# A transformer block on one core: the softmax's sink term added a step later, a merge that begins with other products, and a new order of the last two pairs of products

## The chip, the core and the metric

The kernel runs on one core of a Trainium2 chip. Its engines are TensorE (PE; weight loads are listed apart as PEld), VectorE (DVE), ScalarE (ACT), GpSimd (POOL) and SyncE (SP, which here only issues DMAs). The metric is the time of one execution in microseconds (us) on the device. All times below are us from the start of the profiled span unless something else is said.

## What is computed

One layer over 1024 latent tokens and 256 context tokens of width 1024, everything in fp32: windowed attention with eight query heads on two key/value heads, beside a Fourier mixing; a gated merge of the two; then a gated feed-forward with a convolution of width 3. Cut to what the change touches:

```python
# attention: each block of 128 queries against up to 3 x 128 local keys and 256 context keys
p = softmax(concatenate([s_loc, s_ctx, sink_l], axis=-1), axis=-1)
o = einsum(p_loc, vw) + einsum(p_ctx, v_ctx)          # the sink takes weight and has no value
# merge
m = sigmoid(g_a) * (attn_o @ w_pa) + sigmoid(g_f) * (four_o @ w_pf)
x = x + gt1 * rmsnorm(m @ w_out, g_post1)
# feed-forward, last norm
u, gate = split(modulate(rmsnorm(x, g_pre2), sh2, sc2) @ w_up, 2)
x = x + gt2 * rmsnorm((silu(conv3(u)) * gate) @ w_down, g_post2)
```

## The kernel before, in words

**Products.** Every fp32 product is made of three PE passes: each operand is split into a high and a low half (`split`, L102: ACT copies the high half, `sub` on DVE or POOL forms the low one), and `mm3` (L106) issues high x high, high x low and low x high (L108 to L110). `tt` at L91 is the helper behind every add, subtraction and product of two tiles; nearly all of them run on DVE.

**Attention, about 330 to 517.** A `Unit` is one block of 128 queries of one key/value head (four heads); there are 16, and the digits of a name are block and head: unit 41 is block 4, head 1. `score` makes the scores of one head on PE, adds the mask and takes the row maximum on DVE (`p`, `mx`, L1199). `guard` (L1204) forms `nm`, minus the larger of maximum and sink, and `es` = sink + `nm`. `exp` (L1211) runs on ACT; its call for the first head first exponentiates `es`. `norm` (L1215) adds `es` to the sums, inverts, and scales the four `p` on POOL (L1219). `turn(j)` transposes one key tile of all heads on PE (`pp`, L1224) and splits it (`ph` on ACT, `pl` on DVE); `prod(j)` multiplies the halves with the values into `po` (L1235); `fold` copies half of `po` on ACT (`tp`) and adds it on DVE (`aT`). `step` (L1302) works on three units at once, in six rounds `g`: unit `c` is turned and multiplied, `b` gets its last three exponentials and its norm, `a` its scores, its guard and `exp(0)`. In round 3 the guard of `a` comes last; round 4 begins with `turn(4)` of `c`. The engines run in the order in which the code is written (`manual_schedule`). Each step also carries one product of the Fourier branch (`pf_tile`, result times `sgf`, stored to memory as `mf_d`), and every second step a weight split whose low half (`wlpf`) is made by POOL.

**Merge, from 517.** `PA` lists 16 output tiles `(j, h)`: 128 channels `j`, half `h` of the tokens. Each is a product of 12 matmuls (`pa_mm`), after which `pa_out` multiplies by the gate `sga` and adds `mf` on DVE, and splits the sum. Half `h` = 1 needs `ah`/`al` of the last query blocks. The first two entries are loaded ahead and run at the loop's end (`EARLY`); the loads of entries 2 to 4 are issued behind them, then `att_split(1, ...)` makes the last two `ah`/`al` pairs, and then the other entries follow. SP's queue carries loads and stores in the order in which they are written.

**Down, to the end.** The feed-forward runs in seven products per pair of tiles (P1 to P7, a scheme of Strassen's kind) of 9 or 12 matmuls; the last of them work in three PSUM banks X, Y, Z (`BANK`). X holds P1, P6, P7 and P4, of which ACT copies the first three out (`snP`, L392), each ahead of the next; Y holds P5 and P3. `wino_items` fixes the order: P1, P2, then P4 and P3 of the pair before, then P6, P5, P7; so the last pair's P4 and P3 end the program. Behind a pair's last sums, `finish` squares each half row with its sum (`d_square`, ACT), multiplies by the gate `G2` (`d_gate`, DVE), forms the inverse root in small steps (`rstd_steps`, L160), scales and adds the residual (`d_out`, L1778) and stores. `ssd` holds the sums of squares of the two halves. The last pair (rows i0 = 3 and i1 = 7) has its end written out by hand behind `run(14, M)`.

Of the kernel before, what the change touches and what calls it, by code (L numbers as in the profile page):

```python
# [63 lines left out]
def block_kernel(ctx: ExitStack, tc: tile.TileContext, t: dict, out: bass.AP, dbg: dict):  # L64
# [28 lines left out]
    def add(out, a, b, eng=None):  # L93
        return tt(out, a, b, ALU.add, eng)
# [44 lines left out]
    def tiny(name, n, bufs=4, dtype=F):  # L139
        return small.tile([P, n], dtype, tag=f"ty{n}", name=name, bufs=bufs)  # L140
# [95 lines left out]
    def wino(pairs, items, psf, hooks, slots=False, seng=None):  # L236

# [937 lines left out]
    class Unit:  # L1175
# [186 lines left out]
    with tc.manual_schedule():  # L1362
# [425 lines left out]
    def down_pair(c, m):  # L1788
        last = c == len(CH) - 1
        ld = {p: [d[m] for d in g_d[c, p]] + ([g_both[c, p][m]] if (c, p) in g_both else []) for p in STA}  # L1790

        half = set()

        def finish(i, n):

            first = i not in half
            half.add(i)
            if not first and m == NT // 2 - 1:
                return None

            def squares():
                d_square(i, n)
                d_gate(i, n)
                if first:
                    return None
                rs = rstd_steps(ssd[:, i, :], f"d{i}")
                return [(1, rs[0]), (2, rs[3]), (3, lambda: [rs[1](), d_out(i, 0, rs[2])] and None),
                        (4, lambda: d_out(i, 1, rs[2])), (6, lambda: [d_store(i, h) for h in range(2)] and None)]
            return [(1, squares)]

        def ev(q, pst, sn):
# [9 lines left out]
            y = yd[i, n]  # L1821
            if pst is None:
                add(y, y, sn)
                if last and q == 11:
                    x1_load(m)
                    x1_load(m + NT // 2)
                return None
            add(y, y, pst)
            return finish(i, n) if last else None
# [10 lines left out]
    items = wino_items(len(pairs), START)  # L1840
    pos = {it: k for k, it in enumerate(items)}
# [10 lines left out]
    def load_g2():  # L1852
        for h in range(2):
            G2.append(s(f"G2{h}"))
            load(out=G2[h], in_=gt_d[1, :, h * 512:(h + 1) * 512])

    at(32, lambda: seng.__setitem__(0, nc.gpsimd))
    at(pos[NF - 3, "P1"], lambda: seng.__setitem__(0, nc.vector))
    at(pos[NF - 1, "P3"] + 6, swap_misc)
    at(pos[NF + 12, "P1"], load_g2)  # L1860
    seng = [nc.vector]
    run, ahead, flush, due, pre, conv, sums, mm, evac, st = wino(pairs, items, ps, hooks, True, seng)
    with tc.manual_schedule():
# [200 lines left out]
        i0, i1 = NT // 2 - 1, NT - 1  # L2064
        evac_last = due[M].pop()
        due[M], rest = [], due[M]
        for fn in rest:
            fn()
        d_square(i1, 0)
        rs1 = rstd_steps(ssd[:, i1, :], f"d{i1}")  # L2070
        rs0 = rstd_steps(ssd[:, i0, :], f"d{i0}")
        rs1[0]()
        rs1[3]()
        d_gate(i1, 0)
        rs1[1]()
        assert not evac_last()
        d_square(i0, 1)
        d_out(i1, 1, rs1[2])
        d_store(i1, 1)
        rs0[0]()  # L2080
        rs0[3]()
        d_gate(i0, 1)
        for k in range(7):
            flush(M + k)
        assert not due, sorted(due)
        rs0[1]()
        for i, n, r in ((i0, 1, rs0), (i0, 0, rs0), (i1, 0, rs1)):
            d_out(i, n, r[2])
            d_store(i, n)
    miscD[0].release()  # L2090
# [76 lines left out]
```

## Time and profile before

| what | us |
|---|---|
| three runs, median (lowest to highest) | 1300.64 (1299.89 to 1301.2) |
| the profiled execution, its own time | 1300.34 |
| its span in the trace | 1298.6 |

The span is what the profile shows from the first to the last instruction; 1.74 us of the execution lie around it. The rows further down come from that one execution. PE takes a new matmul before the last has ended, so durations overlap: the distance of two starts is what a matmul costs a full row of them, and a longer distance is a stop. The granted clock of TensorE is 1.00 from 330 to 1265.

### The profile page before, as it was taken

To read this page: it belongs to the slowest core of one execution; us is meant where nothing else is said; L and a number is where in the kernel's file an instruction comes from. 1 tells how busy PE (TensorE), PEld (TensorE's weight loads), DVE (VectorE), ACT (ScalarE), POOL (GpSimd) and SP (SyncE) were. 2 spreads that over 40 slices of the span, in tenths; PEclk is the share of its full clock that TensorE was granted. 3 is DMA by queue.
4 is the path that set the end of the run, shared out by engine and by line. 5 is a ranking of instruction groups with operands and counts; after the bars stand their busy time and mean duration, and the time that the engine had idled before them with its cause. 6 is when DMAs were issued, how large, how long until landed. Compare 5 with 4: busy or idle time off the path is not lost.

```text
span 1298.6 us, 18497 instructions
## 1 busy us (share of the span) xinstructions
PE 1256.2 (97%) x5998; PEld 1022.1 (79%) x5998; DVE 1030.4 (79%) x1865; ACT 682.7 (53%) x1357; POOL 232.0 (18%) x191
## 2 busy tenths in 40 slices
PE   5999999999899999999999999999999999999996
PEld 3768777888878877788878888888888887888884
DVE  4867767875788996867889999999888877666767
ACT  7754337533667676344477555454444555544442
POOL 0001221100333333000000032544554200000000
PEclk9999999999999999999999999999999999999999
DMA  9997474604334343945213686687767778977983
GB/s 317 346 324 232 142 230 138 193 31 134 88 100 120 114 122 110 325 155 157 81 42 106 187 250 210 205 240 222 219 187 227 211 219 288 367 255 222 291 292 140
DMA packets 271573, 254.56 MB, mean 196 GB/s; under 512 B 16732, under 2 KB 206836, under 8 KB 271476
## 3 DMA queue, kind: packets, MB, share of 16 engines
q1 hardware_dynamic: 271476, 253.38, 62.5%
q8 instruction: 47, 0.77, 0.2%
q14 instruction: 50, 0.41, 0.1%
HBM read 179.65 MB, written 73.40 MB: 195 GB/s over the span
## 4 chain that ended last, share of the span: by engine, by line
PE 79%; DVE 13%; ACT 3%; issue 2%; DMA 1%; POOL 1%; SPq 0%; DVEq 0%; POOLq 0%; ACTq 0%
PE X_u L110 5%; PE X_u L109 5%; PE X_u L108 5%; PE X_d L110 3%; PE X_d L109 3%; PE X_d L108 3%; PE Y_u L110 3%; PE Y_u L108 3%; PE Y_u L109 3%; PE X_g L108 2%; PE X_g L109 2%; PE X_g L110 2%; DVE p L1199 2%; DVE pl L91 2%; PE y L110 2%
## 5 line engine op out<-in xcount | busy, mean ns | idle before, releaser
L91 DVE TENSOR_TENSOR lP_u<-A_u,hP_u 128x512 fp32r<-128x512 f32 x132 | 105.7, 805 | 22.6 <-ACT hP_u L330 20.8
L392 ACT COPY snP_u<-X_u 128x512 f32<-128x512 f32 x57 | 33.4, 585 | 128.5 <-PE X_u L110 128.5
L392 ACT COPY snP_d<-X_d 128x512 f32<-128x512 f32 x48 | 28.2, 587 | 97.8 <-PE X_d L110 93.7
L330 ACT CAST hP_u<-A_u 128x512 fp32r<-128x512 f32 x121 | 74.6, 619 | 1.9 <-PE Y_u L109 1.9
L1219 POOL TENSOR_SCALAR p<-p,sm 128x640 f32<-128x640 f32 (+1 forms) x64 | 48.3, 774 | 92.1 <-PE pp L1224 35.3
L103 ACT CAST ph<-pp 128x512 fp32r<-128x512 f32 x76 | 44.3, 584 | 22.3 <-PE pp L1224 21.0
L91 DVE TENSOR_TENSOR pl<-pp,ph 128x512 fp32r<-128x512 f32 x76 | 51.6, 681 | 2.5 <-ACT ph L103 2.0
L91 DVE TENSOR_TENSOR yd<-yd,snP_d 128x512 f32<-128x512 f32 x36 | 24.9, 691 | 34.1 <-ACT snP_d L392 33.9
L1213 ACT ACTIVATE p<-p,nm 128x640 f32<-128x640 f32 (+1 forms) x64 | 51.3, 802 | 0.7 <-DVE nm L1206 0.7
L91 POOL TENSOR_TENSOR A_u<-A_u,A_u 128x512 f32<-128x512 f32 x28 | 48.5, 1732 | 13.8 <-DVE lP_u L91 6.8
L1199 DVE CUSTOM_DVE_ANT_0 p<-ss,mask 128x640 f32<-128x640 f32 (+1 forms) x64 | 49.9, 781 | 0.0
L1224 PE MATMUL pp<-ident,p 128*128 128x128 f32 x304 | 46.6, 274 | 2.8 <-POOL p L1219 1.5
L1224 PEld LDWEIGHTS pp<-ident,p 128*128 128x128 f32 x304 | 37.2, 140 | 11.7 <-POOL p L1219 2.9
L1658 DVE SCALAR_TENSOR_TENSOR tb<-u,vec,tb 128x1024 f32<-128x1024 f32 x22 | 38.8, 1766 | 3.1 <-ACT tb L1655 3.1
L91 POOL TENSOR_TENSOR S_u<-A_u,A_u 128x512 f32<-128x512 f32 x14 | 24.1, 1722 | 89.3 <-DVE u L91 82.2
L1659 DVE SCALAR_TENSOR_TENSOR tb<-u,vec,tb 128x1024 f32<-128x1024 f32 x22 | 37.5, 1704 | 0.9
L1195 PE MATMUL ss<-kst,qs 128*128 128x384 f32 (+1 forms) x128 | 36.6, 367 | 1.3 <-DVE mx L1199 0.8
L91 DVE TENSOR_TENSOR lP_g<-A_g,hP_g 128x512 fp32r<-128x512 f32 x48 | 33.3, 701 | 5.2 <-ACT hP_g L103 4.3
L91 POOL TENSOR_TENSOR A_u<-S_u,A_u 128x512 f32<-128x512 f32 x14 | 18.7, 1333 | 102.6 <-DVE lP_u L91 89.2
L91 DVE TENSOR_TENSOR wB<-wB,wB 128x512 f32<-128x512 f32 x44 | 35.8, 814 | 0.0
L1235 PE MATMUL po<-pl,vst 128*128 128x512 f32 x76 | 31.3, 412 | 3.0 <-DVE pl L91 2.4
L320 ACT COPY snP_g<-X_g 128x512 f32<-128x512 f32 x24 | 14.1, 587 | 36.4 <-PE X_g L110 35.6
(888 smaller groups left out, 4359.5 us busy)
## 6 DMA issues: line engine op xcount, KB each, us to landing
A_u<-in_w_up SPq DMA_DIRECT2D x88, 256.0 KB, 4.4
wB<-in_w_down SPq DMA_DIRECT2D x44, 256.0 KB, 4.4
wa<-in_w_mod SPq DMA_DIRECT2D x36, 256.0 KB, 5.3
wt_dT<-wB SPq DMA_DIRECT2D x33, 256.0 KB, 2.2
wdB<-in_w_down SPq DMA_DIRECT2D x33, 256.0 KB, 4.6
wdT<-wt_dT SPq DMA_DIRECT2D x33, 256.0 KB, 3.1
A_g<-in_w_in SPq DMA_DIRECT2D x32, 256.0 KB, 5.1
ws<-in_w_mod SPq DMA_DIRECT2D x30, 256.0 KB, 6.0
```

Source lines behind the costliest of these rows:

```text
L91: return (eng or nc.vector).tensor_tensor(out=out, in0=a, in1=b, op=op)
L103: copy(hi, src)
L108: nc.tensor.matmul(ps, ah, bh, start=start, stop=False, skip_group_check=True)
L109: nc.tensor.matmul(ps, ah, bl, start=False, stop=False, skip_group_check=True)
L110: nc.tensor.matmul(ps, al, bh, start=False, stop=stop, skip_group_check=True)
L330: copy(st[j]["half", p][0], st[j][STA[p]])
L392: copy(d["s" + p], d["X"])
L1199: nc.vector.tensor_tensor_reduce(out=p_, in0=ssc[:, lo:768], in1=self.mk, op0=ALU.add, op1=ALU.max, scale=1.0, scalar=-3.0e38, accum_out=s ...
L1213: nc.scalar.activation(out=self.pt[g], in_=self.pt[g], func=AF.Exp, scale=SCALE, bias=self.m[:, g:g + 1], accum_out=self.sm[:, g:g + 1])
L1219: nc.gpsimd.tensor_scalar(out=self.pt[g], in0=self.pt[g], scalar1=self.sm[:, g:g + 1], scalar2=1.0, op0=ALU.mult, op1=ALU.mult)
L1224: nc.tensor.transpose(pp[:, g * P:(g + 1) * P], self.pt[g][:, j * P:(j + 1) * P], ident)
L1658: nc.vector.scalar_tensor_tensor(out=tb, in0=u[:, 0:1024], scalar=cw[0], in1=tb, op0=ALU.mult, op1=ALU.add)
```

## The change

There are four pieces. **(1)** The add that forms `es` and its exponential leave `guard` and `exp(0)` and go to a method of their own, `sink`, which `step` calls a step later, in round 1, when the unit has become `b`. **(2)** `PA` begins with the first three tiles of token half 0, then three of half 1. **(3)** `wino_items` runs the last two pairs each by itself, in the order P1, P2, P6, P5, P7, P3, P4; their sums are taken from PSUM one by one. **(4)** `rstd_steps` takes four small DVE operations behind the sums in place of six, one of them ahead of the second sum; `G2` is halved once, with changed sign, on ACT; the hand-written end follows the new order.

```diff
-    def rstd_steps(parts, name):
+    def rstd_steps(parts, name, other=0):
...
+        def early():
+            nc.vector.tensor_scalar(out=w, in0=parts[:, other:other + 1], scalar1=1.0 / D, scalar2=EPS, op0=ALU.mult, op1=ALU.add)
         def one():
-            add(v, parts[:, 0:1], parts[:, 1:2])
-            nc.vector.tensor_scalar(out=v, in0=v, scalar1=1.0 / D, scalar2=EPS, op0=ALU.mult, op1=ALU.add)
+            nc.vector.scalar_tensor_tensor(out=v, in0=parts[:, 1 - other:2 - other], scalar=1.0 / D, in1=w, op0=ALU.mult, op1=ALU.add)
...
-            nc.vector.tensor_scalar(out=n1, in0=n1, scalar1=-0.5, scalar2=1.5, op0=ALU.mult, op1=ALU.add)
-            mul(r2, r, n1)
+            nc.vector.scalar_tensor_tensor(out=r2, in0=n1, scalar=-3.0, in1=r, op0=ALU.add, op1=ALU.mult)
...
+            if i > n - own:
+                items.extend((j, p) for j, p in ([] if i > n - own + 1 else [(i - 1, "P1"), (i - 1, "P2"), (i - 2, "P4"), (i - 2, "P3")]))
+                items.extend((i - 1, p) for p in ("P1", "P2", "P6", "P5", "P7", "P3", "P4") if (i - 1, p) not in items)
+                continue
...
-            self.es, self.sm = tiny(f"es{self.nm}", 4, 16), tiny(f"sm{self.nm}", 4, 16)
-            add(self.es, snk[:, hs], self.m)
+            self.sm = tiny(f"sm{self.nm}", 4, 16)
+
+        def sink(self):
+            self.es = tiny(f"es{self.nm}", 4, 16)
+            add(self.es, snk[:, self.kv * GRP:self.kv * GRP + GRP], self.m)
+            nc.scalar.activation(out=self.es, in_=self.es, func=AF.Exp)
         def exp(self, g):
-            if g == 0:
-                nc.scalar.activation(out=self.es, in_=self.es, func=AF.Exp)
...
             if b and g < 3:
                 b.exp(g + 1)
+                if g == 1:
+                    b.sink()
...
-    PA = ((0, 0), (1, 0), (0, 1), (1, 1)) + tuple((j, h) for j in range(2, KT) for h in range(2))
+    PA = tuple((j, h) for h in range(2) for j in range(3)) + tuple((j, h) for j in range(3, KT) for h in range(2))
...
+    OWN = 2
+    items = wino_items(len(pairs), START, OWN)
...
+        for h in range(2):
+            nc.scalar.activation(out=G2[h], in_=G2[h], func=AF.Copy, scale=-0.5)
...
+        d_square(i1, 0)
+        two0()
+        d_out(i0, 1, r0)
+        d_store(i0, 1)
+        one1()
+        root1()
+        d_gate(i1, 0)
+        two1()
+        d_out(i1, 1, r1)
+        d_store(i1, 1)
+        d_out(i0, 0, r0)
+        d_store(i0, 0)
+        d_out(i1, 0, r1)
+        d_store(i1, 0)
```

How DVE's row of work changes in a step of the attention (unit 31 is `c`, 40 is `b`, 41 is `a`), before, from the guard of unit 41 on:

```order
L1206 SCALAR_TENSOR_TENSOR nm41_4615<-mx41_4539,nsnk_3209 128x4
L91 TENSOR_TENSOR es41_4617<-snk_3188,nm41_4615 128x4
L91 TENSOR_TENSOR pl314_4626<-pp314_4620,ph314_4625 128x512
L91 TENSOR_TENSOR sgf7_4397<-pf7_4564,sgf7_4397 128x512
L91 TENSOR_TENSOR aT10_3228<-po31_4588,tp31_4649 64x2x128 x2
L91 TENSOR_TENSOR pl400_4667<-pp400_4661,ph400_4666 128x512
L1199 ISA p500_4677,mx50_4671<-ss500_4672,mask_3186 128x640
L1199 ISA mx50_4671 128x1
L91 TENSOR_TENSOR pl401_4685<-pp401_4679,ph401_4684 128x512
```

and after, the same stretch and one row more:

```order
L1223 SCALAR_TENSOR_TENSOR nm41_4615<-mx41_4536,nsnk_3209 128x4
L91 TENSOR_TENSOR pl314_4624<-pp314_4618,ph314_4623 128x512
L91 TENSOR_TENSOR sgf7_4394<-pf7_4564,sgf7_4394 128x512
L91 TENSOR_TENSOR aT10_3228<-po31_4588,tp31_4646 64x2x128 x2
L91 TENSOR_TENSOR pl400_4664<-pp400_4658,ph400_4663 128x512
L1216 ISA p500_4674,mx50_4668<-ss500_4669,mask_3186 128x640
L1216 ISA mx50_4668 128x1
L91 TENSOR_TENSOR pl401_4682<-pp401_4676,ph401_4681 128x512
L91 TENSOR_TENSOR es41_4686<-snk_3188,nm41_4615 128x4
```

`es41` no longer stands between `nm41` and `pl314`; it follows `pl401` a step later. POOL's order is the same in both.

DVE's row at the start of the merge, before, from the last two low halves of the attention's output on:

```order
L91 TENSOR_TENSOR al21_5680<-aT11_3229,ah21_5679 128x512
L91 TENSOR_TENSOR al31_5684<-aT11_3229,ah31_5683 128x512
L91 TENSOR_TENSOR sga01_5667<-pa01_5762,sga01_5667 128x512
L91 TENSOR_TENSOR mf01_5668<-mf01_5668,sga01_5667 128x512
L91 TENSOR_TENSOR ml01_5797<-mf01_5668,mh01_5796 128x512
L91 TENSOR_TENSOR sga11_5671<-pa11_5777,sga11_5671 128x512
L91 TENSOR_TENSOR mf11_5672<-mf11_5672,sga11_5671 128x512
L91 TENSOR_TENSOR wlpa4_5814<-wpa4_5775,whpa4_5813 128x512
```

and after:

```order
L91 TENSOR_TENSOR al21_5680<-aT11_3229,ah21_5679 128x512
L91 TENSOR_TENSOR sga20_5667<-pa20_5762,sga20_5667 128x512
L91 TENSOR_TENSOR al31_5684<-aT11_3229,ah31_5683 128x512
L91 TENSOR_TENSOR mf20_5668<-mf20_5668,sga20_5667 128x512
L91 TENSOR_TENSOR ml20_5797<-mf20_5668,mh20_5796 128x512
L91 TENSOR_TENSOR sga01_5671<-pa01_5777,sga01_5671 128x512
L91 TENSOR_TENSOR mf01_5672<-mf01_5672,sga01_5671 128x512
L91 TENSOR_TENSOR wlpa4_5814<-wpa4_5775,whpa4_5813 128x512
```

The gate product of tile (2, 0), `sga20`, has come between `al21` and `al31`; before, both stood ahead of every gate product that was left. On PE tile (2, 0) runs first now, then (0, 1).

DVE's last rows, before, from the sum of P3 of the last pair for row 3 on (`yd31` and `yd71` take the bank Y, `yd70` the bank X):

```order
L91 TENSOR_TENSOR yd31_11557<-yd31_11557,Y_d33_13168 128x512
L1778 SCALAR_TENSOR_TENSOR yd71_11502<-yd71_11502,r2d7_13235,xf71_13090 128x512
L91 TENSOR_TENSOR vd3_13236<-ssd_5759 128x1
L166 TENSOR_SCALAR vd3_13236<-vd3_13236 128x1
L91 TENSOR_TENSOR yd31_11557<-yd31_11557,G21_12600 128x512
L172 RECIPROCAL rd3_13238<-sqd3_13237 128x1
L173 SCALAR_TENSOR_TENSOR n1d3_13239<-rd3_13238,vd3_13236 128x1
L174 TENSOR_SCALAR n1d3_13239<-n1d3_13239 128x1
L91 TENSOR_TENSOR r2d3_13240<-rd3_13238,n1d3_13239 128x1
L1778 SCALAR_TENSOR_TENSOR yd31_11557<-yd31_11557,r2d3_13240,xf31_13086 128x512
L1778 SCALAR_TENSOR_TENSOR yd30_11400<-yd30_11400,r2d3_13240,xf30_13084 128x512
L1778 SCALAR_TENSOR_TENSOR yd70_11545<-yd70_11545,r2d7_13235,xf70_13088 128x512
```

and after, from the sum with which PE's last product (now P4, bank X) is taken on:

```order
L91 TENSOR_TENSOR yd70_11545<-yd70_11545,X_d33_13121 128x512
L175 RECIPROCAL rd3_13160<-sqd3_13159 128x1
L176 SCALAR_TENSOR_TENSOR n1d3_13161<-rd3_13160,vd3_13158 128x1
L177 SCALAR_TENSOR_TENSOR r2d3_13162<-n1d3_13161,rd3_13160 128x1
L1800 SCALAR_TENSOR_TENSOR yd31_11557<-yd31_11557,r2d3_13162,xf31_13140 128x512
L169 SCALAR_TENSOR_TENSOR vd7_13220<-ssd_5759,wd7_13225 128x1
L91 TENSOR_TENSOR yd70_11545<-yd70_11545,G20_12598 128x512
L175 RECIPROCAL rd7_13222<-sqd7_13221 128x1
L176 SCALAR_TENSOR_TENSOR n1d7_13223<-rd7_13222,vd7_13220 128x1
L177 SCALAR_TENSOR_TENSOR r2d7_13224<-n1d7_13223,rd7_13222 128x1
L1800 SCALAR_TENSOR_TENSOR yd71_11502<-yd71_11502,r2d7_13224,xf71_13144 128x512
L1800 SCALAR_TENSOR_TENSOR yd30_11400<-yd30_11400,r2d3_13162,xf30_13138 128x512
```

One row more, the output of `yd70`, ends it. The last addition from PSUM is now `yd70`; it stands ahead of the chain of row 3, and the chain of row 7 (four small rows) behind it. Before it was `yd31`, and the chain behind it had six small rows.

## Rows read from the trace of the kernel before

**Rows 1.** The page's first part: busy time of an engine, its share of the span, and its instructions.

```profile
PE 1256.2 (97%) x5998; PEld 1022.1 (79%) x5998; DVE 1030.4 (79%) x1865; ACT 682.7 (53%) x1357; POOL 232.0 (18%) x191
```

**Rows 2.** The table of stretches, for most of the attention, the start of the merge and what follows it to 640: stretch, its length, then the busy time (and instructions) of PE, PEld, DVE, ACT and POOL, granted clock, DMA share, GB/s.

```profile
363.00:496.00 133.00, 128.36 (x748) 108.05 (x747) 119.14 (x265) 94.32 (x207) 50.47 (x62) 1.00 0.41 119
516.60:523.00 6.40, 4.20 (x16) 2.64 (x15) 5.41 (x10) 2.86 (x5) 0.00 (x0) 1.00 0.70 211
523.00:640.00 117.00, 117.00 (x541) 97.33 (x541) 87.10 (x194) 51.49 (x127) 0.00 (x0) 1.00 0.59 191
```

**Rows 3.** The timelines of POOL and DVE in one step of the attention, 431 to 437: start, duration, engine, line, operation, and in square brackets what the engine waited for before it. `nm`, `es`: guard of unit 41; `pl`: low half of the fifth part of unit 31; POOL's `p` x4: norm of unit 40.

```profile
431.19 3.13 POOL L1219 TENSOR_SCALAR p<-p,sm 128x640 f32<-128x640 f32 x4 [6.83 <-PE po L1235]
...
432.35 0.43 DVE L1206 SCALAR_TENSOR_TENSOR nm<-mx,nsnk 128x4 f32<-128x4 f32 x1
432.81 0.74 DVE L91 TENSOR_TENSOR es<-snk,nm 128x4 f32<-128x4 f32 x1
433.47 0.68 DVE L91 TENSOR_TENSOR pl<-pp,ph 128x512 fp32r<-128x512 f32 x1
...
435.19 1.29 POOL L91 TENSOR_TENSOR wlpf<-wpf,whpf 128x512 fp32r<-128x512 f32 x1 [0.88 <-ACT whpf L103]
```

**Rows 4.** PE's timeline around the fifth `prod` of that step (unit 31), and the same `pp` a step later.

```profile
433.76 0.39 PE L1235 MATMUL po<-ph,vst 128*128 128x512 f32 x1
434.21 0.50 PE L1235 MATMUL po<-pl,vst 128*128 128x512 f32 x1
434.55 0.60 PE L1224 MATMUL pp<-ident,p 128*128 128x128 f32 x4
...
444.60 0.60 PE L1224 MATMUL pp<-ident,p 128*128 128x128 f32 x4
```

**Rows 5.** The view of one tile, `es`, over the whole span: count, duration in ns (min/median/max), first and last start.

```profile
L91 DVE TENSOR_TENSOR es<-snk,nm x16: 161/740/745, 339.1 to 494.9; 128x4 f32<-128x4 f32 x16
```

**Rows 6.** The same view for the tile `al`, whose two operands both lie in SBUF too.

```profile
L91 DVE TENSOR_TENSOR al<-aT,ah x8: 681/688/1365, 445.2 to 521.0; 128x512 fp32r<-128x512 f32 x8
```

**Rows 7.** PE's timeline at the first and at the last of the eleven places where the `po<-pl` behind the guard starts late (their late starts: 384.06, 394.09, 404.13, 414.19, 424.24, 434.21, 444.26, 454.41, 465.76, 475.92, 486.86).

```profile
383.34 0.39 PE L1235 MATMUL po<-ph,vst 128*128 128x512 f32 x1
384.06 0.50 PE L1235 MATMUL po<-pl,vst 128*128 128x512 f32 x1 [0.34 <-DVE pl L91]
...
486.16 0.39 PE L1235 MATMUL po<-ph,vst 128*128 128x512 f32 x1
486.86 0.50 PE L1235 MATMUL po<-pl,vst 128*128 128x512 f32 x1 [0.31 <-DVE pl L91]
```

**Rows 8.** PE's timeline at the two steps that wait at the next unit's first transposes as well.

```profile
458.89 0.66 PE L1224 MATMUL pp<-ident,p 128*128 128x128 f32 x4 [0.53 <-DVE pl L91]
...
480.40 0.66 PE L1224 MATMUL pp<-ident,p 128*128 128x128 f32 x4 [0.76 <-DVE pl L91]
```

**Rows 9.** PE's timeline where it waits for POOL's norm, in two steps that follow each other.

```profile
364.51 0.33 PE L1224 MATMUL pp<-ident,p 128*128 128x128 f32 x1 [0.34 <-POOL p L1219]
...
374.18 0.33 PE L1224 MATMUL pp<-ident,p 128*128 128x128 f32 x1 [0.44 <-POOL p L1219]
```

**Rows 10.** DVE's timeline ahead of the loop of steps: the `es` of unit 01.

```profile
353.91 0.73 DVE L91 TENSOR_TENSOR es<-snk,nm 128x4 f32<-128x4 f32 x1
```

**Rows 11.** PE's timeline at the start of the merge: `pa01`, from its first matmul, and its stops.

```profile
516.59 0.39 PE L108 MATMUL pa<-ah,whpa 128*128 128x512 f32 x1
517.68 0.50 PE L109 MATMUL pa<-al,whpa 128*128 128x512 f32 x1 [0.70 <-DVE al L91]
...
519.83 0.50 PE L108 MATMUL pa<-ah,whpa 128*128 128x512 f32 x1 [0.72 <-ACT ah L103]
521.10 0.50 PE L109 MATMUL pa<-al,whpa 128*128 128x512 f32 x1 [0.78 <-DVE al L91]
```

**Rows 12.** The timelines of SP's queue (issues only) and of DVE there.

```profile
517.46 0.65 SPq L1329 DMA_DIRECT2D sga<-sga_d  x1
...
520.36 1.29 DVE L91 TENSOR_TENSOR al<-aT,ah 128x512 fp32r<-128x512 f32 x2
```

**Rows 13.** The view of the DMAs from 517.4 to 518.15, the list of issues: what, engine, operation, count, KB, median us from issue to landing.

```profile
sga<-sga_d SPq DMA_DIRECT2D x1, 256.0 KB, 4.2
```

**Rows 14.** The view of the tile `sga` from 490 to 560, its last line: its loads from issue to landing.

```profile
DMA to landing us min/median/max: 3.5/5.1/5.8
```

**Rows 15.** PE's timeline at the end: the last matmul of the last pair's P7, the first of its P4 and of its P3, and the last one of all.

```profile
1281.56 0.39 PE L110 MATMUL X_d<-dT,lP_d 128*128 128x512 f32 x1
1282.63 0.50 PE L108 MATMUL X_d<-dT4n,hP_d 128*128 128x512 f32 x1 [0.68 <-ACT snP_d L392]
...
1286.11 0.50 PE L108 MATMUL Y_d<-dB,hP_d 128*128 128x512 f32 x1 [1.15 <-DVE yd L91]
...
1288.06 0.39 PE L110 MATMUL Y_d<-dB,lP_d 128*128 128x512 f32 x1
```

**Rows 16.** DVE's timeline at the end: the last addition from PSUM, the last step of the last norm chain, and the three last outputs.

```profile
1289.41 0.68 DVE L91 TENSOR_TENSOR yd<-yd,Y_d 128x512 f32<-128x512 f32 x1
...
1292.38 0.16 DVE L91 TENSOR_TENSOR r2d<-rd,n1d 128x1 f32<-128x1 f32 x1
1292.57 2.08 DVE L1778 SCALAR_TENSOR_TENSOR yd<-yd,r2d,xf 128x512 f32<-128x512 f32 x3
```

**Rows 17.** ACT's timeline among the last products, a copy out of a bank behind a long wait, near the place of the two new operations on `G2`.

```profile
1235.07 0.59 ACT L392 COPY snP_d<-X_d 128x512 f32<-128x512 f32 x1 [4.16 <-PE X_d L110]
```

More of the change, by code (lines that the diff above doesn't have):

```diff
@@ L173, in two @@
             nc.vector.scalar_tensor_tensor(out=n1, in0=r, scalar=v, in1=r, op0=ALU.mult, op1=ALU.mult)
-            nc.vector.tensor_scalar(out=n1, in0=n1, scalar1=-0.5, scalar2=1.5, op0=ALU.mult, op1=ALU.add)
-            mul(r2, r, n1)
-        return one, two, r2, root
+            nc.vector.scalar_tensor_tensor(out=r2, in0=n1, scalar=-3.0, in1=r, op0=ALU.add, op1=ALU.mult)
+        return early, one, root, two, r2
     def transpose8(xn, psf, name):
@@ L224, in block_kernel, with wino_items @@
     FIRST = {"P1", "P5", "P2"}
-    def wino_items(n, start=()):
+    def wino_items(n, start=(), own=0):
         items = list(start)
         for i in range(n + 1):
+            if i > n - own:
+                items.extend((j, p) for j, p in ([] if i > n - own + 1 else [(i - 1, "P1"), (i - 1, "P2"), (i - 2, "P4"), (i - 2, "P3")]))
+                items.extend((i - 1, p) for p in ("P1", "P2", "P6", "P5", "P7", "P3", "P4") if (i - 1, p) not in items)
+                continue
+            if own and i == n - own:
+                continue
             for p in ("P1", "P2", "P4", "P3", "P6", "P5", "P7"):
@@ L234, in wino_items, with wino @@
         return items
-    def wino(pairs, items, psf, hooks, slots=False, seng=None):
+    def wino(pairs, items, psf, hooks, slots=False, seng=None, own=0):
         st = [dict() for _ in pairs]
@@ L394, in run2 @@
                         at_item(k + 1, lambda ev=ev, q={"P1": 11, "P6": 12, "P7": 22}[p], x=d["s" + p]: ev(q, None, x))
+                if j >= len(pairs) - own:
+                    q = {"P2": (11, "Z"), "P3": (12, "Y"), "P4": (21, "X"), "P5": (22, "Y")}.get(p)
+                    if q:
+                        first_at(k + 1, lambda d=d, ev=ev, q=q: ev(q[0], d[q[1]], None))
+                    continue
                 q = {"P2": (11, "Z", "sP1"), "P3": (12, "Y", "sP6"), "P4": (21, "X", None), "P7": (22, "Y", "sP7")}.get(p)
@@ L1379, in block_kernel @@
         u0.exp(0)
+        u0.sink()
         u0.exp(1)
@@ L1790, in down_pair, with gate @@
         ld = {p: [d[m] for d in g_d[c, p]] + ([g_both[c, p][m]] if (c, p) in g_both else []) for p in STA}
-        half = set()
+        done = {}
         def finish(i, n):
[L1796 to L1799, printed above, removed]
+            first = i not in done
+            if first:
+                done[i] = rstd_steps(ssd[:, i, :], f"d{i}", n)
             def squares():
                 d_square(i, n)
+            def gate():
                 d_gate(i, n)
[L1804 to L1809, printed above, removed]
+            if first:
+                return [(1, squares), (2, gate), (2, lambda: done[i][0]() and None)]
+            if m == NT // 2 - 1:
+                last_two[i] = done[i]
+                return None
+            early, one, root, two, r2 = done[i]
+            return [(1, squares), (2, lambda: [one(), root(), gate()] and None), (3, lambda: [two(), d_out(i, 0, r2)] and None),
+                    (4, lambda: d_out(i, 1, r2)), (5, lambda: [d_store(i, h) for h in range(2)] and None)]
+        seen = set()
         def ev(q, pst, sn):
@@ L1821, in ev @@
             y = yd[i, n]
[L1822 to L1829, printed above, removed]
+            if last and not seen:
+                x1_load(m)
+                x1_load(m + NT // 2)
+            add(y, y, sn if pst is None else pst)
+            two_sums = q == 21 or q in seen
+            seen.add(q)
+            return finish(i, n) if last and two_sums else None
         return ev, ld
+    last_two = {}
     hb, mov = {}, {}
@@ L1860, in block_kernel @@
     at(pos[NF + 12, "P1"], load_g2)
+    at(pos[NF + 12, "P1"] + 4, half_g2)
     seng = [nc.vector]
-    run, ahead, flush, due, pre, conv, sums, mm, evac, st = wino(pairs, items, ps, hooks, True, seng)
+    run, ahead, flush, due, pre, conv, sums, mm, evac, st = wino(pairs, items, ps, hooks, True, seng, OWN)
     with tc.manual_schedule():
@@ L2064, in block_kernel @@
         i0, i1 = NT // 2 - 1, NT - 1
[L2065 to L2068, printed above, removed]
-        d_square(i1, 0)
[L2070 to L2073, printed above, removed]
+        _, one0, root0, two0, r0 = last_two[i0]
+        last_sum, gate1, early1 = due.pop(M)
+        d_square(i0, 1)
+        gate1()
+        early1()
+        one0()
+        root0()
+        d_gate(i0, 1)
+        last_sum()
+        _, one1, root1, two1, r1 = last_two[i1]
+        d_square(i1, 0)
+        two0()
[3 more added lines that the diff above has]
+        root1()
         d_gate(i1, 0)
[L2075 to L2078, printed above, removed]
+        two1()
+        d_out(i1, 1, r1)
         d_store(i1, 1)
[L2080 to L2084, printed above, removed]
+        d_out(i0, 0, r0)
+        d_store(i0, 0)
+        d_out(i1, 0, r1)
+        d_store(i1, 0)
         assert not due, sorted(due)
[L2086 to L2089, printed above, removed]
     miscD[0].release()
```

6 lines of the change are left out of this document (4 added, 2 removed).

## The prediction, made before the run

> **What bounds the kernel now.** I read the page's first part, then the table of stretches, then PE's timeline wherever a stretch is not full. PE is busy for 97% of the span [rows 1], so whatever doesn't end a stop of PE, or shorten what follows PE's last matmul, is worth nothing. From 523 to 640 PE is busy for 117.00 of 117.00; the attention leaves 4.64 of 133.00 open, and the first 6.40 of the merge leave 2.20 [rows 2]. The end, where DVE finishes what PE no longer does, is the third place. Behind a stop PE pays a little more than the gap: the matmul that starts again lasts 0.50 in place of 0.39 and the next one starts 0.34 later in place of 0.23 [rows 4], so I add 0.11 for each stop. Units of 0.227 for a matmul come from the last product: nine matmuls of which the first pays 0.34 start within 1.95 [rows 15], so (1.95 - 0.34) / 7 = 0.23.
>
> **The sink term.** It removes an add of 128x4 from the place between `nm` and the fifth `pl`. That add is small, yet it takes 0.74 of a microsecond at the median, and 0.161 at its least [rows 5]. In the step shown POOL scales four `p` from 431.19 for 3.13, that is 0.78 each, with ends at 431.97, 432.75, 433.53 and 434.32; `es` starts at 432.81, just behind the second end, and is over at 433.55, just behind the third [rows 3]. So it sits out one of POOL's instructions. `al`, whose operands also lie in SBUF, goes from 0.69 to 1.37 at its longest [rows 6].
>
> The Trainium skill has a rule for it ("SBUF — State Buffer", Who interferes with whom): a DVE instruction with two SBUF inputs contends with a GpSimd instruction that reads SBUF, and the later one is blocked until the other ends. Rows 3 agree. By that rule the same add costs as much wherever POOL is at work, so the change gains only if POOL rests at the new place; that is the third rival.
>
> Who waits: `pl` is queued behind `es` on DVE and would start at 432.81 in place of 433.47, 0.66 earlier. PE's `po<-pl` starts at 434.21, 0.45 behind the matmul before it; 0.22 of that is a stop [rows 4]. There are eleven such stops. The first is 0.72 - 0.23 = 0.49, the last 0.70 - 0.23 = 0.47 [rows 7]; the eleven gaps add up to 3.89, and with 11 x 0.11 to **5.1**. None is over 0.52, less than the 0.66, so all should go.
>
> What is late next? A steady step takes 444.60 - 434.55 = 10.05 [rows 4]; less 0.27 and 0.11, a usual stop, it would take 9.67. Where PE waits for POOL's norm in two steps running, the period is 374.18 - 364.51 = 9.67 as well [rows 9]. So POOL's chain (exponentials, sum, norm, transposes) is the next limit at about the new period. It gets shorter itself, since the first exponential no longer waits on ACT behind `es`. I take the whole 5.1 and let half of it stay in the lower bound.
>
> Two steps stop at the next unit's transposes besides, for 0.69 and 0.92 [rows 8] (their waits are put at 0.53 and 0.76 behind DVE's `pl`). DVE comes 0.66 earlier there and ACT's part of the chain 0.2 more, 0.87 together, while the step itself starts some 0.49 earlier, a mean stop; so about 0.4 of each stop goes, **0.8**. Ahead of the steps `es` of unit 01 takes 0.73 of DVE's time too [rows 10], ahead of the sums that POOL's norm needs, and at 364.51 PE waits for that norm [rows 9]. Between 0 and 0.66 I take **0.4**, the nearer end by that wait of PE. The add at its new place, behind `pl401` in DVE's row, stands in a stretch in which POOL rests: some 3.7 into the step, about 438.2, between the end of `wlpf` (435.19 + 1.29 = 436.48) and the next norm, 10.05 behind 431.19 [rows 3]. At 0.16 it delays the scores behind it; as no stop of PE is known there I take **-0.3** for all of them, with 0 as the other end. The exponential of `es` keeps its 0.2 on ACT, which has slack in round 1. Sum: 5.1 + 0.8 + 0.4 - 0.3 = **6.0**, bounds 3.0 (half of the stops stay, a little of the rest) and 7.3 (the odd steps give 1.6 and unit 01 all of 0.66).
>
> **The merge's order.** Before, `pa01` stops for 1.09 - 0.23 = 0.86 with 0.11 behind it, then 0.89 and 1.05 + 0.11 [rows 11]: 3.02. Now `pa20` runs first. Its `ah`/`al` are of token half 0 and long made, so it fills 12 x 0.227 = 2.72, from 516.59 to 519.31. `pa01` then wants `al21` with its eighth matmul at 520.90 and gets it when the first of the two `al` ends, about 521.05 [rows 12]: a stop of 0.20 + 0.11. The next is new. In DVE's row `sga20` now stands between `al21` and `al31`, and `sga20` needs a load which SP issues at 517.46 [rows 12]; the load issued there lands 4.2 later [rows 13], at 521.66. Behind it `sga20` 0.60 and `al31`, which then is done at about 523.04, when PE wanted it at 521.87: 1.2 + 0.11. That leaves stops of 1.62, a gain of 3.02 - 1.62 = **1.4**. Loads of `sga` land after 3.5 to 5.8 [rows 14]. At 3.5 DVE doesn't wait, `al31` is done at 522.25 and the gain is 2.2; at 5.8 it is -0.2; the break-even is a landing at about 523.1. Since PE is full from 523 on [rows 2], what is gained stays.
>
> **The end.** In the last pair PE stops ahead of P4 for the copy of P7 out of the same bank (1282.63 - 1281.56 - 0.23 = 0.84, and 0.11) and ahead of P3 for DVE's sum out of bank Y (nine matmuls after 1282.63 the gap is 1286.11 - 1284.58 - 0.23 = 1.31, and 0.11) [rows 15]: 2.37. In the new order every copy or sum out of a bank has a product of 9 x 0.227 = 2.04 in another bank to itself, against 0.59 for a copy and 0.69 for an add, so both stops go. DVE's row has little to spare there: put row after row at 0.60 for an add, 0.67 for an output and 0.2 for a small one, the sum out of Y that P3 wants at 1281.8 is done at 1281.7; if DVE is 0.3 later, PE stops for 0.2. Behind PE: the last addition from PSUM starts at 1289.41, 0.96 behind the end of PE's last matmul (1288.06 + 0.39), as a norm chain stands ahead of it on DVE [rows 15, 16]; by the new row it starts some 0.4 sooner. Two small steps of the last chain, each 0.19 from start to start (1292.38 to 1292.57), are gone: 0.4. The three last outputs, 2.08 [rows 16], stay behind the last chain, and their stores with them. Sum: 2.37 + 0.4 + 0.4 = **3.2**, bounds 2.0 (only the stops, less a new one) and 3.5.
>
> The halving of `G2` is two ACT operations over 128x512, 0.6 each by the copy of that size, near a place where ACT waits for 4.16 [rows 17], and they let two small DVE operations of each chain be one; at nothing. Without that cover a copy out of PSUM would be 1.2 late, still inside a product of 2.04. On SP the first stores of the last pairs' rows now stand ahead of some later weight loads. Both stops at the end are put down to ACT and DVE [rows 15], none to a load; at nothing, and a load that came late would cost what it is late.
>
> **The sum.** 6.0 + 1.4 + 3.2 = 10.6. The profiled execution took 1300.34, of which 1.74 lie around the span; 1300.34 - 10.6 = 1289.7. The median is 0.3 above it: 1290.0. I forecast **1289.9**.
>
> **The rivals.**
> - *The attention gains little.* POOL's chain at 9.67 [rows 9] or another one takes over the stops. For it: DVE is busy for 119 of 133 [rows 2], the tightest after PE. Against it: `es` stands in that chain as well. It leaves about 1 of the 6.0: 1300.3 - 5.6 = 1294.9. Chance 0.12.
> - *The merge or the end doesn't do what it says.* `sga20`'s load lands at 5.8, or DVE is late for P3: 6.0 + 0 + 2.2 = 8.2, so 1292.3. Chance 0.09.
> - *Slower.* The add meets an instruction of POOL at the new place in every step. If it sits out one like `wlpf` (1.29), POOL's chain takes 9.67 + 1.2 = 10.87 a step, 0.8 more than now; 13 steps make +10.6, less 4.6 of merge and end: +6, 1306. It decides from a block of 0.73 a step: 13 x (9.67 + 0.73 - 10.05) = 4.6. Against it: POOL rests for nearly 5 there [rows 3]. Chance 0.03.
>
> **How the numbers follow.** The forecast has 0.74, with 1287.0 (bounds 7.3, 2.2 and 3.5 nearly together) to about 1292; the remaining 0.02 is for what I have not seen. The range goes to 1294.5, which takes in the second rival and part of the first. A measurement of this kernel tells 0.2% (2.6 us) from no change: faster by more has 0.92 (forecast and two rivals, less what of them ends near nothing), same 0.05, slower 0.03.
>
> **What would show it.** In the profile after: `es` at about 160 ns at the median, if the reason is right; no stop at `po<-pl` behind the guard, and steps of about 9.7; `pa20` without a stop from the merge's start, then one stop of over 1 us in `pa01` while DVE waits for the load of `sga`; no stop in the last 15 us of PE, and PE's end, counted back from DVE's last output, some 5.4 before it. I am wrong if `es` still takes 0.7, if steps stay at 10.05 with PE waiting for POOL, or if `pl`, though early, is not what PE waited for.

## The result, and the profile after

| what | before | after |
|---|---|---|
| median of runs, us | 1300.64 (1298.79 to 1301.51) | 1288.8 (1288.42 to 1290.92) |
| ratio, 95% interval | | 0.9912 [0.9901, 0.9924] |
| span of the profiled execution | 1298.6 | 1287.3 |

By the ratio the changed kernel takes 11.4 us less; 10.6 less, 1289.9, was forecast. I read the two profiles in the three places of the forecast. The table of stretches of the profile after, with columns as in [rows 2]:

```profile
363.00:490.00 127.00, 125.11 (x743) 108.02 (x744) 111.34 (x263) 95.43 (x206) 49.65 (x61) 1.00 0.43 125
514.00:520.00 6.00, 4.63 (x20) 3.19 (x19) 4.11 (x8) 0.62 (x2) 0.00 (x0) 1.00 0.94 318
520.00:640.00 120.00, 120.00 (x555) 99.89 (x554) 91.19 (x212) 56.80 (x146) 0.00 (x0) 1.00 0.55 177
```

In the attention PE is idle for 1.89 of 127 instead of 4.64 of 133 [rows 2]; behind 520 PE is full, as before. The tile `es`, as in [rows 5], and one step on POOL, DVE and PE, as in [rows 3, 4]:

```profile
L91 DVE TENSOR_TENSOR es<-snk,nm x16: 150/152/154, 339.3 to 497.9; 128x4 f32<-128x4 f32 x16
...
428.33 3.14 POOL L1238 TENSOR_SCALAR p<-p,sm 128x640 f32<-128x640 f32 x4 [6.41 <-PE po L1254]
...
429.49 0.44 DVE L1223 SCALAR_TENSOR_TENSOR nm<-mx,nsnk 128x4 f32<-128x4 f32 x1
429.85 0.68 DVE L91 TENSOR_TENSOR pl<-pp,ph 128x512 fp32r<-128x512 f32 x1
...
435.04 0.15 DVE L91 TENSOR_TENSOR es<-snk,nm 128x4 f32<-128x4 f32 x1
...
430.92 0.39 PE L1254 MATMUL po<-ph,vst 128*128 128x512 f32 x1
431.15 0.39 PE L1254 MATMUL po<-pl,vst 128*128 128x512 f32 x1
431.38 0.27 PE L1243 MATMUL pp<-ident,p 128*128 128x128 f32 x1
...
441.04 0.60 PE L1243 MATMUL pp<-ident,p 128*128 128x128 f32 x4
```

`es` is never slow now: none of its 16 adds overlaps an instruction of POOL. `pl` follows `nm` at once, `po<-pl` follows `po<-ph` after 0.23, and the step takes 441.04 - 431.38 = 9.66. The merge's start on PE, DVE and SP, as in [rows 11, 12]:

```profile
510.29 0.39 PE L108 MATMUL pa<-ah,whpa 128*128 128x512 f32 x1
...
514.80 0.50 PE L109 MATMUL pa<-al,whpa 128*128 128x512 f32 x1
...
517.09 0.50 PE L109 MATMUL pa<-al,whpa 128*128 128x512 f32 x1 [1.33 <-DVE al L91]
...
514.06 0.69 DVE L91 TENSOR_TENSOR al<-aT,ah 128x512 fp32r<-128x512 f32 x1
515.75 0.69 DVE L91 TENSOR_TENSOR sga<-pa,sga 128x512 f32<-128x512 f32 x1 [1.00 <-DMA sga<-sga_d]
516.35 0.68 DVE L91 TENSOR_TENSOR al<-aT,ah 128x512 fp32r<-128x512 f32 x1
...
511.16 0.38 SPq L1350 DMA_DIRECT2D sga<-sga_d  x1
```

The second `al` stands behind the gate product `sga`, which waits 1.00 for its load: the new stop that was forecast. The end on PE (the first P3 matmul of the last pair and the last of all) and DVE, as in [rows 15, 16], and the list of DMA issues from 1280 on:

```profile
1274.24 0.39 PE L110 MATMUL X_d<-dT,lP_d 128*128 128x512 f32 x1
1274.47 0.47 PE L108 MATMUL Y_d<-dB,hP_d 128*128 128x512 f32 x1
...
1278.43 0.39 PE L110 MATMUL X_d<-dT4n,lP_d 128*128 128x512 f32 x1
...
1278.98 0.68 DVE L91 TENSOR_TENSOR yd<-yd,X_d 128x512 f32<-128x512 f32 x1
...
1282.20 2.08 DVE L1800 SCALAR_TENSOR_TENSOR yd<-yd,r2d,xf 128x512 f32<-128x512 f32 x3
...
out<-yd SPq DMA_DIRECT2D x4, 256.0 KB, 2.1
```

PE's two stops are gone but for 0.08 behind 1274.47. The span ends 3.02 behind DVE's last output (1284.28); before it was 3.95 (1298.6 - 1294.65). In the profile before, the stores of the end and the last output of the pair before the last look like this (timelines of SP's queue and of DVE, and the list of DMA issues from 1290.5 on):

```profile
1290.78 4.47 SPq L1781 DMA_DIRECT2D out<-yd  x8
...
1286.57 0.75 DVE L1778 SCALAR_TENSOR_TENSOR yd<-yd,r2d,xf 128x512 f32<-128x512 f32 x1
...
out<-yd SPq DMA_DIRECT2D x8, 256.0 KB, 2.8
```

The four outputs of the pair before the last are done by 1287.32, but their stores stand in SP's queue behind the first store of the last pair, whose output ends at 1290.75; so all eight go out from 1290.78 on, one right behind the other.

The 11.3 between the two spans are made up as follows. The attention gives 516.59 - 510.29 = **6.3**. From there to the first full stretch it is **1.1** (stops of 1.92 in place of 3.02). To PE's last matmul it is **2.2** (1288.06 - 1278.43 = 9.63, less 7.4). From PE's last matmul to DVE's last output it took 6.20 before and 5.46 after, **0.74**. The rest, behind DVE's last output, is **0.93**.

### The profile page after: what moved, and what is told of

It is laid out like the page before. It is cut to its first block, busy times and chain, and to the rows that moved or that the text cites. A ratio compares the mean times of both kernels' runs of the same rounds, so it can differ in the third digit from the quotient of the medians.

```text
span 1287.3 us, 18499 instructions
## 1 busy us (share of the span) xinstructions
PE 1252.8 (97%) x5998; PEld 1023.0 (79%) x5998; DVE 1022.3 (79%) x1857; ACT 686.5 (53%) x1359; POOL 232.1 (18%) x191
## 4 chain that ended last, share of the span: by engine, by line
PE 84%; DVE 7%; ACT 3%; DMA 2%; issue 2%; POOL 1%; SPq 1%; DVEq 0%; POOLq 0%; ACTq 0%
PE X_u L110 5%; PE X_u L108 5%; PE X_u L109 5%; PE X_d L108 3%; PE X_d L109 3%; PE X_d L110 3%; PE Y_u L108 3%; PE Y_u L110 3%; PE Y_u L109 3%; PE X_g L108 2%; PE X_g L110 2%; PE X_g L109 2%; PE pp L1243 2%; PE y L109 2%; PE y L110 2%; PE y L108 2%
## 5 line engine op out<-in xcount | busy, mean ns | idle before, releaser
L1684 ACT ACTIVATE tb<-tb 128x1024 f32<-128x1024 f32 x22 | 23.4, 1062 | 18.5 <-DVE tb L1681 18.5
```

## The experiments

Each ratio is to runs of the kernel before on the same chip and is followed by its 95% interval; the differences in us are worked out from the ratio, of about 1300, unless a median is named.

**The three parts, each alone on the kernel before.** `e1_sink_alone` takes piece (1), `e2_merge_alone` piece (2), `e3_end_alone` pieces (3) and (4) of the diff above.

> The kernel before with the sink term a step later and nothing else of the change. My theory (the add sits out an instruction of POOL at its old place and holds up the row behind it on DVE): it shows the attention's share as the profile after gave it, from 516.59 to 510.29 at the merge's start, so about 6.3 less than before, 1294.3; es about 0.15 in the median. Rival (part of those 6.3 came from the merge's loads, which the change also moved): 3 to 5.

> The kernel before with the new order of the merge's tiles and nothing else. Theory: 3.02 of stops become 0.2 + 0.11 and a wait for the load of sga20, as in the profile after (1.92 in all): 1.1 less, 1299.5. Rival (the load lands earlier or later when the attention ends later): between -0.2 and 2.2 less; the place to look at is DVE's wait ahead of sga20.

> The kernel before with the last two pairs by themselves and the shorter norm chains, and nothing else. Theory: two stops of PE (2.37) go, DVE's last output ends 0.7 to 0.8 sooner behind PE, and the last store is issued and lands 0.9 sooner, as in the profile after: 3.9 less, 1296.7. Rival (the 0.9 behind the last output is not of this piece but chance of one execution): 3.0 less, 1297.6.

Sink alone: 0.9963 [0.9951, 0.9975], 4.8 less; `es` 152 ns in the median. By time that lies with the rival (3 to 5), though 6.3 is inside the interval; the traces decide, further down. Ten of the eleven stops are gone from its trace, and the last is 0.22. Merge alone: 0.999 [0.9982, 0.9999], 1.3 less; its stops are 0.22 and 0.89 with 0.11 each, 1.3 in all in place of 3.02. End alone: 0.9976 [0.9966, 0.9985], 3.1 less; the time is the rival's (3.0), but the trace has the 0.9: DVE's last three outputs are

```profile
1290.46 2.08 DVE L1795 SCALAR_TENSOR_TENSOR yd<-yd,r2d,xf 128x512 f32<-128x512 f32 x3
```

and end at 1292.54 of a span of 1295.6, 3.06 ahead of its end, so the 0.9 belong to this piece. That execution, whose time is also the median, lost 1.6 at the merge to a lower clock (last section). The three sum to 9.2 where the whole is 11.4; the intervals leave that open, so I took the sink's move out of the whole:

```diff
-            self.sm = tiny(f"sm{self.nm}", 4, 16)
+            self.es, self.sm = tiny(f"es{self.nm}", 4, 16), tiny(f"sm{self.nm}", 4, 16)
+            add(self.es, snk[:, hs], self.m)
...
```

> The changed kernel with the sink term put back into the guard, merge and end as changed. The three parts apart gave 4.8, 1.3 and 3.1 by their ratios, 9.2 together, the whole 11.4. If the parts add up as the traces of one execution have it (6.3 for the attention), this takes 1295.1; if the attention's part is 4.8, 1293.6; if the parts help one another, more than 1295.5 is possible.

0.9958 [0.9946, 0.9971], 5.5 less than before and so 5.9 from the whole; the eleven stops (383.00 to 485.83) are back, and `es` takes 0.74. So the sink's part is 4.8 by one comparison and 5.9 by the other, and 6.3 by the two profiles, for which the noise of both leaves room; that the parts help one another isn't shown.

**Why the add was slow.** The add stays at its old place, and one operand is read from PSUM.

```diff
+            if g == 3:
+                self.sp = ssc[:, 768:772]
+                copy(self.sp, snk[:, self.kv * GRP:self.kv * GRP + GRP])
...
-            add(self.es, snk[:, hs], self.m)
+            add(self.es, self.sp, self.m)
```

> The kernel before with the add of the sink term left at its old place, but its sink operand read from PSUM: one more ACT copy of 128x4 for each unit puts it into the unused columns of the scores' bank. Theory (the add is slow since both operands lie in SBUF while POOL reads SBUF): es takes 0.2 or less, the stops at po<-pl go or shrink below 0.1, and the time falls by 4 to 6, to 1295 to 1297. Rival (the add is slow at that place for another reason, such as its dependence on nm or POOL's writes): es stays near 0.74 and the time within 1 of 1300.6.

0.9955 [0.9943, 0.9967], 5.9 less. The tile `es`, then POOL and DVE in one step:

```profile
L91 DVE TENSOR_TENSOR es<-ss,nm x16: 160/161/164, 338.8 to 489.3; 128x4 f32<-128x4 f32 x16
...
438.23 2.35 POOL L1222 TENSOR_SCALAR p<-p,sm 128x640 f32<-128x640 f32 x3 [4.96 <-PE po L1238]
...
439.39 0.43 DVE L1209 SCALAR_TENSOR_TENSOR nm<-mx,nsnk 128x4 f32<-128x4 f32 x1
439.85 0.16 DVE L91 TENSOR_TENSOR es<-ss,nm 128x4 f32<-128x4 f32 x1
```

The add runs in 0.16 in the middle of POOL's norm, at the very place where it took 0.74; 14 of the 16 adds lie inside one of POOL's `p`, and none takes more than 0.164. None of the eleven stops is left. `nm` ahead of it, with both operands in SBUF, still takes 0.43 and ends at 439.82, just behind POOL's second end (438.23 + 2 x 0.78 = 439.79). So it was the pair of SBUF operands, not the place or what the add depends on. The rule of the Trainium skill ("SBUF — State Buffer", Who interferes with whom), that a DVE instruction with two SBUF inputs contends with a GpSimd instruction that reads SBUF, holds here, and one operand in PSUM ends it.

**Is DVE's chain or PE the next limit?** The same for `nm`, on the changed kernel. This kernel and the ones that follow were timed in other groups of runs than the change, so beside the medians it counts that the ratios' intervals of `e7_nm_psum`, `e5_early_load`, `e6_stores_bunched` and `e8_long_chains` all contain the change's 0.9912: what each of them gives or costs is told by its trace.

```diff
+            if g == 3:
+                self.sp = ssc[:, 768:772]
+                copy(self.sp, nsnk[:, self.kv * GRP:self.kv * GRP + GRP])
...
-            nc.vector.scalar_tensor_tensor(out=self.m, in0=self.mx, scalar=-SCALE, in1=nsnk[:, hs], op0=ALU.mult, op1=ALU.min)
+            nc.vector.scalar_tensor_tensor(out=self.m, in0=self.mx, scalar=-SCALE, in1=self.sp, op0=ALU.mult, op1=ALU.min)
```

> The changed kernel with one operand of nm read from PSUM, one more ACT copy of 128x4 for each unit. nm still takes 0.43 and ends just behind one of POOL's instructions in the profile after, on the way from the last maximum to the fifth pl and to the first exponential. Theory (in a steady step PE has become full at 9.67, so that a shorter chain on DVE gives nothing there): nm takes 0.25 or less, steps stay at 9.67, the time within 0.8 of 1288.8. Rival (POOL's chain sets 9.67, and nm stands in it): 0.2 to 0.27 less in each of 13 steps, 3 less, 1286.

Median 1287.78, 0.9899 [0.9882, 0.9915], 1.0 less than the change's median. The tile, and two successive steps:

```profile
L1226 DVE SCALAR_TENSOR_TENSOR nm<-mx,ss x16: 148/157/159, 338.6 to 487.8; 128x4 f32<-128x4 f32 x16
...
428.88 0.16 DVE L1226 SCALAR_TENSOR_TENSOR nm<-mx,ss 128x4 f32<-128x4 f32 x1
438.55 0.16 DVE L1226 SCALAR_TENSOR_TENSOR nm<-mx,ss 128x4 f32<-128x4 f32 x1
```

`nm` is 0.27 shorter and the step is still 9.67: PE is full there, and the rival (3 less) falls. About 0.7 are `nm`'s own, ahead of the steps and in the odd ones (the table further down); its merge stop was 0.95 in place of 1.50, which `nm` has no part in.

**The merge's new stop.** The load of tile (2, 0) goes with the first two.

```diff
-                for jh in PA[:2]:
+                for jh in PA[:3]:
...
-    for jh in PA[2:5]:
+    for jh in PA[3:5]:
```

> The changed kernel with the gate and the partial sum of the merge's third tile (2, 0) loaded together with the first two, a step ahead of the end of the attention. In the profile after, DVE waits 1.00 for that load ahead of sga20, and PE stops 1.50 + 0.11 for al31 behind it. Theory (the load is what al31 waits for): DVE doesn't wait, al31 is done some 1.2 sooner, the stop shrinks to 0.3 to 0.5, and the time falls by about 1.1, to 1287.7. Rival (al31 waits for its place behind sga20 on DVE in any case, or the earlier loads push others back): the same time within 0.5.

Median 1287.55, 0.99 [0.9881, 0.9919], 1.3 less than the change's. DVE and PE:

```profile
517.50 1.29 DVE L91 TENSOR_TENSOR al<-aT,ah 128x512 fp32r<-128x512 f32 x2
518.82 0.69 DVE L91 TENSOR_TENSOR sga<-pa,sga 128x512 f32<-128x512 f32 x1
...
518.24 0.50 PE L109 MATMUL pa<-al,whpa 128*128 128x512 f32 x1
```

Only the stop of 0.21 + 0.11 is left. The order of the rows changed with the load: both `al` now run ahead of the gate product. So the second stop goes (1.50 + 0.11 in the profile after), but how much is the load and how much the row isn't told apart. The profiled execution is the slowest of its four, 1290.71, for reasons outside the merge: it lost 2.2 ahead of the attention (last section) and 1.2 in the attention's last step.

**The end: stores and chains.** In the first kernel four stores are put back behind the first one of the end; in the second, apart from that, the norm chains are the long ones, in the new order of products.

```diff
         d_store(i0, 1)
+        for i in held:
+            for h in range(2):
+                d_store(i, h)
...
```

> The changed kernel with the four stores of the last pair but one put behind the store of row 3's second half, in SP's queue, as the kernel before had four stores behind the first one of its end. Theory (the 0.9 that the end gained behind DVE's last output, 3.02 to the span's end in place of 3.95, is that eight stores no longer crowd into the last 4.5 us: issues of 0.33 in place of 0.58, landing after 1.7 in place of 2.35): the span ends 3.9 to 4.0 behind DVE's last output again, and the time is 0.9 longer, 1289.7. Rival (that 0.9 comes with another thing, such as the clock after PE's end): it stays at 3.0.

Median 1289.42, 0.6 above the change's; its ratio, 0.9912 [0.9896, 0.9929], is the same. Its trace decides: DVE's last output ends at 1282.85 and the span at 1287.3, 4.45 behind, in place of 3.02. DVE's last outputs, SP's queue and the list of DMA issues from 1279 on:

```profile
1280.77 2.08 DVE L1800 SCALAR_TENSOR_TENSOR yd<-yd,r2d,xf 128x512 f32<-128x512 f32 x3
...
1279.57 4.46 SPq L1803 DMA_DIRECT2D out<-yd  x8
...
out<-yd SPq DMA_DIRECT2D x8, 256.0 KB, 2.8
```

Eight stores take 2.8 from issue to landing, where four took 2.1. The 4.45 is more than the 3.9 to 4.0 that I expected: the last store is issued 0.58 behind DVE's end, since each issue takes up to 0.6, where in the kernel before it was 0.02; without that it would be 3.9 again.

```diff
-            nc.vector.scalar_tensor_tensor(out=r2, in0=n1, scalar=-3.0, in1=r, op0=ALU.add, op1=ALU.mult)
+            nc.vector.tensor_scalar(out=n1, in0=n1, scalar1=-0.5, scalar2=1.5, op0=ALU.mult, op1=ALU.add)
+            mul(r2, r, n1)
...
```

> The changed kernel with the norm chains of before (six small operations behind the last sum of squares, none ahead, the gate not halved), the new order of the products kept. Theory (two small operations of 0.19 each behind the last sum, and what the second chain ahead of it adds on DVE): DVE's last output ends 5.8 to 6.0 behind PE's last matmul in place of 5.46, and the time is 0.4 longer, 1289.2. Rival (the chains are covered by other rows of DVE): the same within 0.1 in the profile.

Median 1289.23, 0.9908 [0.9892, 0.9924]. PE's last matmul and DVE's last rows:

```profile
1277.92 0.39 PE L110 MATMUL X_d<-dT4n,lP_d 128*128 128x512 f32 x1
...
1282.24 0.16 DVE L91 TENSOR_TENSOR r2d<-rd,n1d 128x1 f32<-128x1 f32 x1
1282.43 2.08 DVE L1802 SCALAR_TENSOR_TENSOR yd<-yd,r2d,xf 128x512 f32<-128x512 f32 x3
```

DVE ends 1284.51 - 1278.31 = 6.20 behind PE, more than the 5.8 to 6.0 that I expected and just what it was before the change, so the whole 0.74 is the chains'.

**Both additions together**, the early load and `nm` from PSUM:

> The changed kernel with both of the last ideas: the early load of the merge's third tile and nm with one operand from PSUM. By the traces of the two apart, the first takes away a stop of 1.6 in the merge and the second 0.4 in the attention: 2.0 less than 1288.8, 1286.8. Rival (one of the two was an execution's chance): 1287.5 to 1288.5.

1286.04 (1285.6 to 1286.2), 0.9892 [0.9876, 0.9907]: 14.0 less than before, 2.8 under the change's median, 2.6 by the ratios, and the best of all kernels here. Not all of it is the two additions': in the profiled execution PE is 1.0 earlier already ahead of the attention, at the last `pab` (342.97 in place of 343.96).

**One measure over all traces.** Two profiles alone mix what a change does with what differs from one execution to the next. So here are three distances from PE's timeline of every run on which the argument rests: from the last matmul of `pab` (a product of the Fourier branch ahead of the steps) to the last of `po`; the stop in the attention's last step, which is 1.08 before and 0.29 after; and the second stop of the merge.

```profile
507.24 0.51 PE L1235 MATMUL po<-pl,vst 128*128 128x512 f32 x1 [0.91 <-DVE pl L91]
...
500.88 0.50 PE L1254 MATMUL po<-pl,vst 128*128 128x512 f32 x1
```

| kernel | `pab` to last `po` | last step's stop | the first less the second | second merge stop |
|---|---|---|---|---|
| before | 172.32 | 1.08 | 171.2 | old order |
| `e2_merge_alone` | 171.61 | 0.29 | 171.3 | 0.89 |
| `e3_end_alone` | 171.51 | 0.29 | 171.2 | old order |
| `e10_no_sink_move` | 172.06 | 0.77 | 171.3 | 0.91 |
| the change | 166.09 | 0.29 | 165.8 | 1.50 |
| `e1_sink_alone` | 165.87 | 0.28 | 165.6 | old order |
| `e5_early_load` | 167.35 | 1.47 | 165.9 | none |
| `e6_stores_bunched` | 165.85 | 0.28 | 165.6 | 1.10 |
| `e8_long_chains` | 165.99 | 0.29 | 165.7 | 0.86 |
| `e7_nm_psum` | 165.56 | 0.62 | 164.9 | 0.95 |
| `e9_load_and_nm` | 165.68 | 0.69 | 165.0 | none |

Without the last step's stop the four kernels with the old sink lie within 0.1 of each other, and the five with its move alone in the attention within 0.3: the move gives 171.3 - 165.7 = 5.6, alone as in the whole, so the rival of `e1_sink_alone` falls. The stop in the last step is small or large with either, so as far as these traces tell it goes with the execution and not with the move; what sets it is open. The second merge stop of the profile after is the longest of six.

## Why the prediction was right, point by point

- **Sink term, 6.0 forecast, 5.6 measured over the traces.** The cause is shown by the operand in PSUM. Ten of the eleven stops went, and the last became smaller (counted whole, 5.1). The odd steps stop for 0.21 and 0.50 in place of 0.69 and 0.92 (0.9, forecast 0.8), the wait at 364.51 moved to 363.99 (0.5, forecast 0.4). The loss was 0.9, not 0.3: what is left of the eleventh stop at 480.93 (0.23 + 0.11), and new stops at 461.59 (0.27) and 481.87 (0.29). The two profiles differ by 6.3 since they hold, besides, the stop in the last step, 1.08 and 0.29, which I hadn't counted and which doesn't follow the move.
- **The next limit.** I named POOL's chain at 9.67. In a steady step it is PE itself, as the shorter `nm` shows; that the 9.67 of the first steps [rows 9] agreed was luck, for it is another quantity: in the profile after it is 373.56 - 363.99 = 9.57.
- **Merge, 1.4 forecast, 1.1 measured.** The mechanism was right, and the size hung on the landing, as said: the load landed 4.5 behind its issue in place of 4.2, `al31` was done at 517.03, and the stop is 1.50 in place of 1.2. In the five other traces with this order and load it is 0.86 to 1.10, which makes the gain 1.5 to 1.7.
- **End, 3.2 forecast, 3.9 measured.** The two stops gave 2.2 of 2.37. Behind PE it was 0.74 of 0.8, but half of it for another reason: I gave 0.4 to the addition that starts sooner. It does start sooner, 0.16 behind PE and not 0.96, but the chain that stood ahead of it now stands behind, which is the same; both shorter chains count. The order of the stores on SP I put at nothing, by looking at waits of PE alone: that was the step that failed. The stores decide what follows DVE's last output, and their new order is worth 0.9.
- **The nearness of the sum, 10.6 to 11.3 of the spans, is in part luck.** The stores' 0.9 and the 0.8 of the last step's stop, neither of them forecast, stand against a loss that I took 0.6 too small and a long merge stop in that execution. Two slips are small: `al31` would be done at 522.95 by its own terms, not 523.04, and 1300.3 - 5.6 is 1294.7; the rivals' 1294.9 and 1292.3 hold 0.2 that lies between 1289.7 and the forecast.
- The three rivals fell: steps shortened by 0.4, merge and end gave 5.0, and the add met no instruction of POOL.

## What to carry to other kernels

A tiny instruction that takes many times its shortest duration is a row to look for; compare its end with the ends of the other engines' instructions before moving it, and consider reading an operand from PSUM instead. Where a queue issues stores in the order in which they are written, one that waits holds back those behind it that are ready; here they then landed together at the end of the program. When rows are reordered, look at which load the new first row needs. And a stop that two profiles show at different lengths may be chance: look for it in a third.

## What the runs showed of the hardware that I had not expected

- Stores that follow each other closely take longer to issue: of the eight of `e6_stores_bunched`, one right behind the other, the first takes 0.34, the second 0.42 and the eighth 0.60; the last three of the profile after, 0.66 apart from start to start, take 0.33 each. The landing goes from 2.1 to 2.8 in the median. Why isn't shown.
- In the profile of `e3_end_alone`, which keeps the three stops of the merge, TensorE's granted clock fell behind them; in that of `e5_early_load` it fell behind a stop of 2.4 ahead of the attention. The stretches before and with the fall, for each:

```profile
516.00:520.40 4.40, 2.47 (x8) 1.53 (x9) 4.32 (x8) 2.46 (x5) 0.00 (x0) 1.00 0.67 196
520.40:524.00 3.60, 3.60 (x10) 2.78 (x9) 1.40 (x3) 0.47 (x1) 0.00 (x0) 0.53 0.96 329
...
320.00:326.20 6.20, 4.16 (x19) 3.09 (x17) 0.96 (x4) 1.22 (x2) 0.00 (x0) 1.00 0.94 247
326.20:329.60 3.40, 3.17 (x15) 3.17 (x16) 0.61 (x2) 1.22 (x2) 0.00 (x0) 0.50 0.90 312
```

In the first, PE had been busy for 2.47 of 4.40; then the clock was 0.53, near the lower level of 1.2 GHz, and nine matmuls lost 0.2 each at most, 1.6 in all. In the second, PE had been busy for 4.16 of 6.20; then the clock was 0.50, and with the longer stop that execution was 2.2 behind the profile after. No other profile here shows a fall at either place. The kernel before has the same three stops at the merge, and before and after stop for 1.4 where `e5_early_load` stops for 2.4. How often it happens is open.
